# One RWKV-7 layer with its feed-forward network: new durations and offsets for the list scheduler, and new tile sizes

## The chip, the cores and the metric

The program runs on one core of a Trainium2 chip. The metric is the device time of one execution in microseconds (us). The kernel before took 2997.66 us in the median of three runs (2985.98 to 2998.62).

A core has five engines that are spoken of here: TensorE (PE in the profile; its weight loads are PEld), VectorE (DVE), ScalarE (ACT), GpSimd (POOL) and SyncE (SP), which issues most of the DMA transfers. Each engine works its own list of instructions in order, and waits for the others by semaphores. SBUF is the on-chip memory: 128 partitions, and a tile has the same byte address in each of its partitions. PSUM holds the results of PE.

## The reference

One layer over 2048 tokens of width 1024: RWKV-7 time mixing with 16 heads of 64, a layer norm, a gated feed-forward network (FFN) of width 2816 with a causal convolution of width 3, and a second layer norm.

```python
def step(state, inp):                       # per head, 64 x 64, one token after the other
    r_t, w_t, k_t, v_t, kk_t, a_t = inp
    sa = jnp.einsum('bhij,bhj->bhi', state, -kk_t)
    state = (state * w_t[:, :, None, :] + sa[..., None] * (kk_t * a_t)[:, :, None, :]
             + v_t[..., None] * k_t[:, :, None, :])
    return state, jnp.einsum('bhij,bhj->bhi', state, r_t)

# mixed = ((head_norm(y) + bonus) * gate) @ w_o
x = _layer_norm(DEEPNORM_ALPHA * x + mixed, ln1_g[i], ln1_b[i])
# hdn = conv3(x @ w_in) + conv_b; u, g = split(hdn); ffn = (silu(g) * u) @ w_out
x = _layer_norm(DEEPNORM_ALPHA * x + ffn, ln2_g[i], ln2_b[i])
```

`r`, `k` and `v` are projections of the token-shifted input with 1024 x 1024 weights; the decay `w`, `a` and the gate come from low-rank pairs. All data are fp32.

## The kernel before

**Arithmetic.** A large fp32 product is made of three matmuls in the type fp32r on a high and a low part of each operand: `mm3` (L139 to L143) issues high by high (L141), high by low (L142 or L143) and low by high. In the profile such a matmul is `out<-weights,moving`, or with the two names the other way round. Each takes 128 x 128 weights and streams 512 columns.

**Stages.** One list of nodes holds the whole kernel:

- stage A (0 to about 700 us): projections k, r and v with their low-rank parts. A weight matrix is held in two column halves: half h = 0 in the pool `a_w0`, half h = 1 in `a_w1`. A group of PE is 24 matmuls `ps<-WH,xiH`, `ps<-WL,xiH`, `ps<-WH,xiL`.
- recurrence (about 690 to 1294 us): 16 chunks of 128 tokens, in two halves of the heads and two subchunks of 64 tokens. For each half: a load `l`, a cumulative sum `csI` on PE, exponentials `P`, `Pe`, `Pi` on ACT (L823), products `l<-l,P` (L845), `l<-l,Pe` (L841) and `BKn` (L891) on DVE, transposes `tb` (L899), the Gram products `G` on PE and their masking `Gm` (L917). Then the triangular inversion of the chunk: 31 steps on DVE, each a product `itmp` (L949) and a subtraction `XU` (L954). Its result goes to DRAM (`XD`) and back transposed (`XT`), and `X` (L983) feeds the merge on PE (`mp`). The state goes through `UV`, `Z`, `Zs`, `SA`, `dS`, and is updated on DVE by `stmp` (L1098) and `state` (L1103).
- group norm, gate and output projection (about 1293 to 1503 us), 16 token tiles of 128: sums of squares on ACT (`junk`, L1241, 16 for each tile), rsqrt on DVE, the gate product `wE` (L1270, L1273), transposes to `yE` or `yH`/`yL`, and groups of 24 matmuls `z`.
- FFN (1503 to 2978 us): four blocks of 512 tokens; 44 groups of 24 matmuls `ps<-xH,wiH`, `ps<-xL,wiH`, `ps<-xH,wiL` for each block, and 44 groups of 12 matmuls `acc` for each, the second product.

**What sets the order.** Every node is added by `pl.add(engine, duration, priority, function, dependencies, take, give)`. `order()` plays the list through before the program is built: an engine that is free takes the ready node with the smallest priority number whose slots (`take`: buffers and PSUM banks) are free, holds the engine for the duration, and releases dependents after the duration and a fixed latency. The order in which nodes start in this play is the order in which each engine's instructions are written. So the durations, and the priorities, which are a stage's base time plus an offset from the tables `TS` (recurrence) and `TW` (output projection), decide the order, and nothing else; the instructions stay the same. In `TS`, `b` is 23.2 times the chunk number, and the offsets used with it are `inv` (the inversion, L922), `mrg` and `mc` (the merge, L965 and L967), `uv` (the load of `UV`, L1030), `st` and `cs` (the state, L1034); `e0` is taken off for chunk 0. In `TW`, the base is `p0` plus 13 times the token tile, and `st`, `gt`, `tr` and `out` are the offsets of the squares, the gate, the transposes and the output of the layer norm.

**Where the tiles lie.** Tiles come from SBUF pools opened with `tc.tile_pool`, which lays them one behind the other. In the program as built, these are the byte addresses modulo 64 of the operands of the 512-column matmuls: `xH`, `xL`, `xiH`, `xiL` and the weights of half h = 1 in stage A at 0; `wiH`, `wiL`, `woH`, `woL`, `aH`, `aL`, `yH`, `yL` and the weights of half h = 0 at 32; `yE` at 0.

Of the kernel before, what the change touches and what calls it, by code (L numbers as in the profile page):

```python
# [11 lines left out]
F32 = mybir.dt.float32  # L12
# [105 lines left out]
class K:  # L118
# [3 lines left out]

    def ld(self, out, in_):
        return self.nc.sync.dma_start(out, in_)

    st = ld
# [31 lines left out]
    def run(self, phases="ASWF", scratch=None):  # L158
        tc, nc, a = self.tc, self.nc, self.a
        with ExitStack() as ctx:  # L160
# [24 lines left out]
            self.ident = top.tile([128, 128], F32, name="ident")  # L185
# [21 lines left out]
    def a_nodes(self, ctx, pl):  # L207
# [5 lines left out]
        E = lambda **kw: st2.enter_context(tc.tile_pool(reuse_waits="tile", **kw))  # L213
# [8 lines left out]
        E = lambda **kw: st1.enter_context(tc.tile_pool(reuse_waits="tile", side="right", **kw))  # L222
# [41 lines left out]
        for sw, (q, wi, mm, ml) in enumerate((("k", 1, 2, 4), ("r", 0, 0, 1), ("v", 2, 3, 5))):  # L264
# [73 lines left out]
            for h in range(2):  # L338
# [25 lines left out]
                else:  # L364
# [21 lines left out]
                    l2n.append(pl.add("ACT", 0.4, pr + 0.1, fb, [n2], give=("stg",)))  # L386
# [14 lines left out]
            def front(g):  # L401
# [85 lines left out]
                n_l1 = pl.add("PE", 4.33 if q == "v" else 1.93, lp, f_l1, pn + l1n, take=("ph",),  # L487
# [11 lines left out]
                if q == "v":  # L499
# [13 lines left out]
                    n_h = pl.add("ACT", 1.5, lp, f_sg, [n_ha], take=("hid",), give=("ph",))  # L513
                    n_hid = [pl.add("DVE", 0.65, lp, f_gl, [n_h], give=("hz",))]
                else:
# [11 lines left out]
                    n_h = pl.add("ACT", 0.9 if q == "r" else 0.6, lp, f_hid, [n_ha, n_ones], take=("hid",))  # L527
                    n_hid = [n_h, pl.add("DVE", 0.35, lp, f_hl, [n_h], give=("hz",))]
# [7 lines left out]
            for nq, (g, h, tl) in enumerate(order):  # L536
# [6 lines left out]
                if True:  # L543
                    c = slice(h * 512, h * 512 + 512)
                    if True:
# [17 lines left out]
                        if nq < o["ks"][sw] or q == "v" and nq >= len(order) - o["ke"]:  # L563
                            for u in range(3):
                                n_mm = pl.add("PE", 1.29, (wt if sw == 0 else pr) + 0.2 * u, lambda u=u, f=f_mm: f(u),
                                              [n_mm, pn[u], wn[h, 2 * u], wn[h, 2 * u + 1]], take=() if u else (f"pg{pg}",))
                        n_mm = pl.add("PE", 1.29 if n_mm else 5.14, pr, lambda u=3 if n_mm else None, f=f_mm: f(u),
# [15 lines left out]
                        n_l2 = pl.add("PE", 0.86 if q == "v" else 0.43, pr + 0.1, f_l2, n_hid + l2n, take=("pl",),  # L583
# [14 lines left out]
                        if q == "k":  # L598
# [29 lines left out]
                            hn.append(pl.add("ACT", 2.15, po + 0.5, f_ss, [n_kr] + hn))  # L628
# [101 lines left out]
    TS = dict(hf=12, T=23.2, lds=5.0, hs=8.9, inv=31.0, mrg=66.3, mc=4.0, uv=47.5, st=70.2, cs=17.6, e0=30.0, p0=-3.4, fill=(), fn=1,  # L730
# [3 lines left out]
    def s_nodes(self, ctx, pl, n_1, n_2, w, f):  # L734
# [14 lines left out]
        def f_open1():  # L749

            nonlocal inv, wkp, ldp, pw, xui, triI, gmask, cols, gm4, nbI, nbIn, nbE, scE
            E = lambda st=pools1, **kw: st.enter_context(tc.tile_pool(reuse_waits="tile", side="right", **kw))
# [50 lines left out]
        for t in range(NT):  # L803
# [4 lines left out]
            for h in range(2):  # L808
# [47 lines left out]
                n_pp = pl.add("PE", 0.44, hb + 0.7, f_pcp, [n_P, n_R], take=("pw",), give=("P",))  # L856
# [6 lines left out]
                for i, n_x in ((0, n_M), (1, n_R)):  # L863
# [17 lines left out]
                    n_t = pl.add("PE", 0.44, hb + 0.9 + 0.3 * i, f_tr, [n_x], take=("pw",))  # L881
# [4 lines left out]
                for c in range(2):  # L886
# [17 lines left out]
                    n_tb = pl.add("PE", 0.44, hb + 2.0 + c, f_tb, n_bks[2 * c:2 * c + 2], take=("pw",))  # L904
                    n_bt = pl.add("ACT", 0.6, hb + 2.1 + c, f_bt, [n_tb], take=("BKT",), give=("pw",))
# [8 lines left out]
                    n_g = pl.add("PE", 1.05, hb + 2.2 + c, f_g, [n_bt] + evs, take=("pw", "pw"), give=("BKT",))  # L914
# [51 lines left out]
            for c in range(2):  # L966
# [51 lines left out]
                n = pl.add("DVE", 0.67, mc, f_x11, [n_xt], take=("X11",))  # L1018
                n_m1 = pl.add("PE", 0.45, mc, f_m1, [n], take=("mp",), give=("X11",))
                n = pl.add("ACT", 0.6, mc, f_ft, [n_m1], take=("FT",), give=("mp",))  # L1020
                n = pl.add("PE", 0.68, mc, f_m2, [n], take=("mp",), give=("FT",))
                n_x12.append(pl.add("ACT", 0.6, mc, f_x12, [n], give=("mp",)))
                n_ga.append(pl.add("ACT", 1.0, mc + 0.5, f_ga, [n_m1, n_nu]))
# [9 lines left out]
            for c in range(2):  # L1033
# [21 lines left out]
                n_y1 = pl.add("PE", 1.27, sb + 4, f_y1, prevS + evs + ars[0] + [n_z2], take=("Y",))  # L1055
                for u in range(nh):
# [48 lines left out]
                    n_s0 = pl.add("ACT", 1.04 * d, sp, f_s0, (prevS if nh == 1 or len(prevS) < 2 else prevS[u:u + 1]) + [n_uv])  # L1105
                    n_z = pl.add("PE", 1.27 * d, sp, f_z, [n_s0, n_ga[c]], take=bk)
                    n_zs.append(pl.add("ACT", 0.48 * d, sp, f_zs, [n_z, prevA] + n_zs[-1:]))
                    n_sa = pl.add("PE", 1.27 * d, sp, f_sa, n_zs[-1:] + [n_x12[c]], give=(f"XT{c}",) if lastu else ())
                    n_su.append(pl.add("ACT", 0.96 * d, sp, f_su, [n_sa]))
                    n_ds = pl.add("PE", 1.27 * d, sp, f_ds, n_su[-1:])  # L1110
                    n_w.append(pl.add("DVE", 0.6 * d, sp, f_w, [n_ds, *prevS] + n_w[-1:], give=bk))
                    n_s1.append(pl.add("DVE", 0.6 * d, sp, f_s1, n_w[-1:] + n_s1[-1:] + [prevY] + pcs))
                n_y2 = pl.add("PE", 1.27, sb + 4.5, f_y2, n_su + [n_y1] + (n_s1 if c else []),
                              give=("AR", "BKn", "Gm", "PC", "UV") if c else ())
                n_yt = pl.add("ACT", 0.96, sb + 5, f_yt, [n_y2], take=() if c else ("Yt",), give=("Y",))
# [25 lines left out]
    TW = dict(ne=4, st=-31.5, gt=-31.1, tr=-14.5, ld=-22.0, out=26.9, p0=1000.0,  # L1141
# [3 lines left out]
    def w_nodes(self, ctx, pl, n_first, n_ch1, xds, Q, n_rest, stores, f):  # L1145
# [12 lines left out]
        def f_open(early):  # L1158
            E = lambda st=ctx, **kw: st.enter_context(
                tc.tile_pool(reuse_waits="tile", side="right" if early else "left", **kw))  # L1160
# [59 lines left out]
        def loads(t):  # L1220
# [22 lines left out]
            for i in range(8):  # L1243
                n = pl.add("ACT", 0.54, PR(t) + o["st"], lambda i=i: f_ss(i), [n], take=() if i else ("w_q",))
# [42 lines left out]
        def transposes(x, nm, src, pr, deps, early, give=()):  # L1287
            out = []
            for u in range(2):
# [7 lines left out]
                n = pl.add("PE", 0.44, pr + 0.1 * u, f_t, deps + [n_late] * (e == "L") + [n for n, _ in out],  # L1297
# [41 lines left out]
        for t in range(NT):  # L1339
# [4 lines left out]
            for h in range(2):  # L1344
                e = bank("pz", t < 1)
                if t < 2:

                    n = zn[-1][0] if h else None
                    for k in range(KD):
                        n = pl.add("PE", 0.65, pr + 0.1 * k + 5.2 * h,  # L1350
# [3 lines left out]
                else:  # L1354
                    n = pl.add("PE", 5.14, pr + 5.2 * h, lambda t=t, h=h, e=e: [f_mm(t, h, k, e) for k in range(KD)],
# [50 lines left out]
    def f_nodes(self, ctx, pl, Q, n_early, n_w, n_rest, zs, gn, n_sx, n_x1):  # L1406
# [19 lines left out]
        def f_mid():  # L1426
            E = lambda **kw: ctx.enter_context(tc.tile_pool(reuse_waits="tile", side="right", **kw))
# [4 lines left out]
        def f_rest():  # L1432
            E = lambda **kw: ctx.enter_context(tc.tile_pool(reuse_waits="tile", side="left", **kw))
# [28 lines left out]
        for B in range(NB):  # L1462
# [40 lines left out]
            def wout(f, h, pr, mm=True, acc_mm=acc_mm, abank=abank, an=an, accs=accs):  # L1503
# [20 lines left out]
                if 0 < f < NF - 1:  # L1524
                    accs[h] = [pl.add("PE", 2.56, pr, lambda: [acc_mm(f, h, tl, R["H"], R["L"]) for tl in range(4)],
# [3 lines left out]
                for tl in range(4):  # L1529
                    out.append(pl.add("PE", 0.64, pr + 0.1 * tl, lambda tl=tl: acc_mm(f, h, tl, R["H"], R["L"]),  # L1530
# [4 lines left out]
            for f in range(NF):  # L1535
# [3 lines left out]
                for j, fc in enumerate((f, NF + f)):  # L1539
# [24 lines left out]
                    n_mm = pl.add("PE", 5.14, pr, f_mm, [n_w] + xn, take=("w_" + e,), give=("f_wi",))  # L1564
# [128 lines left out]
            for tl in range(4):  # L1693
                n = pl.add("PE", 3.84, pr, lambda tl=tl: [m(tl) for m in mm], nw + [an[f] for f in range(NF)] + [n])
# [69 lines left out]
```

## Time and profile before

| what | value |
|---|---|
| median of three runs | 2997.66 us (2985.98 to 2998.62) |
| the profiled execution's own time | 2995.38 us |
| its span, first to last instruction | 2993.6 us |
| granted PE clock over the span | 0.968 of full speed |
| PE busy | 2828.6 us, 94% |
| DVE busy | 2066.9 us, 69% |
| ACT busy | 1702.8 us, 57% |

The span is what the engines show between their first and last instruction; the 1.8 us around it belong to the execution's time. Busy times are unions over the span, so that overlapping matmuls count once. [...]

### The profile page before, as it was taken

What the parts mean: (1) busy time and instruction counts of PE and PEld (TensorE: products, weight loads), DVE (VectorE), ACT (ScalarE), POOL (GpSimd) and SP (SyncE); (2) the same over time, 40 slices, a digit from 0 to 9 for tenths busy, and PEclk for the clock granted to TensorE, in tenths of its full rate; (3) what the DMA queues carried; (4) which work ended last, traced back from release to release, by engine and by line L of the source; (5) the groups of instructions that cost most, each with busy time, mean ns of one, the idle gap of its engine ahead of it and who ended that gap; (6) DMA issues with size and microseconds to landing.
All of it is one profiled execution on the core that took longest, in us unless ns stands there. A gap on an engine that the chain in (4) does not pass through costs nothing.

```text
span 2993.6 us, 51468 instructions
## 1 busy us (share of the span) xinstructions
PE 2828.6 (94%) x19392; PEld 2290.7 (77%) x19392; DVE 2066.9 (69%) x4160; ACT 1702.8 (57%) x4604; POOL 52.6 (2%) x94
## 2 busy tenths in 40 slices
PE   7999999998788888799999999999999999999997
PEld 5776778886576777678888887888878888888886
DVE  7888768986899888778765555475554744547454
ACT  8888567663576667777554444444444444444441
POOL 0000000001000000001100000000000000000000
PEclk9999999998899889799999999999999999999999
DMA  6346555435555555468553223242232422424222
GB/s 203 140 166 231 174 182 192 145 117 167 146 151 146 151 157 156 119 231 286 199 179 99 91 93 126 95 147 97 94 124 95 151 92 88 129 94 157 89 87 78
DMA packets 267319, 424.04 MB, mean 142 GB/s; under 512 B 120672, under 2 KB 146272, under 8 KB 262976
## 3 DMA queue, kind: packets, MB, share of 16 engines
q1 hardware_dynamic: 255744, 379.87, 40.2%
q0 software_dynamic: 11328, 40.90, 3.8%
q8 instruction: 152, 2.49, 0.4%
q14 instruction: 95, 0.78, 0.1%
HBM read 311.57 MB, written 109.12 MB: 141 GB/s over the span
## 4 chain that ended last, share of the span: by engine, by line
issue 55%; PE 20%; DVE 10%; ACT 8%; DMA 5%; POOL 1%; SPq 0%; POOLq 0%; ACTq 0%; DVEq 0%
PE ps L141 4%; PE ps L142 4%; PE ps L143 4%; ACT junk L619 3%; DVE BKn L891 2%; DMA l<-in 1%; DVE itmp L949 1%; DVE XU L954 1%; PE G L744 1%; DVE Gm L917 1%; DMA NU<-Gm 1%; DMA NUs<-NU 1%; DMA stg<-in_w_rkv_dram 1%; PE csI L744 1%; ACT UV L743 1%
## 5 line engine op out<-in xcount | busy, mean ns | idle before, releaser
L143 PE MATMUL ps<-xH,wiL 128*128 128x512 f32 x1408 | 557.8, 396 | 0.5 <-DVE wiL L1552 0.4
L141 PE MATMUL ps<-xH,wiH 128*128 128x512 f32 x1408 | 556.8, 395 | 0.0
L142 PE MATMUL ps<-xL,wiH 128*128 128x512 f32 x1408 | 556.7, 395 | 0.0
L1552 DVE TENSOR_TENSOR wiL<-wis,wiH 128x1024 fp32r<-128x1024 f32 x176 | 215.4, 1224 | 488.2 <-ACT wiH L1413 488.2
L1413 ACT ACTIVATE hb<-ps 128x512 f32<-128x512 f32 x176 | 105.6, 600 | 518.2 <-PE ps L143 518.2
L141 PE MATMUL ps<-WH,xiH 128*128 128x512 f32 x768 | 307.7, 401 | 15.5 <-ACT xiH L231 10.0
L143 PEld LDWEIGHTS ps<-xH,wiL 128*128 128x128 f32 x1408 | 264.6, 188 | 65.6 <-DVE wiL L1552 2.1
L142 PEld LDWEIGHTS ps<-xL,wiH 128*128 128x128 f32 x1408 | 264.4, 188 | 63.7
L141 PEld LDWEIGHTS ps<-xH,wiH 128*128 128x128 f32 x1408 | 264.5, 188 | 62.9
L142 PE MATMUL ps<-WL,xiH 128*128 128x512 f32 x768 | 305.2, 397 | 2.0 <-DVE WL L326 2.0
L143 PE MATMUL ps<-WH,xiL 128*128 128x512 f32 x768 | 304.9, 397 | 0.0
L1580 DVE SCALAR_TENSOR_TENSOR cv<-hb,cw,cv 128x512 f32<-128x512 f32 x352 | 263.5, 749 | 20.7 <-ACT cv L1576 14.5
L142 PE MATMUL acc<-woL,aH 128*128 128x512 f32 x688 | 269.2, 391 | 1.6 <-DVE woL L1517 1.6
L143 PE MATMUL acc<-woH,aL 128*128 128x512 f32 x688 | 269.8, 392 | 0.0
L141 PE MATMUL acc<-woH,aH 128*128 128x512 f32 x688 | 268.4, 390 | 0.0
L1413 ACT ACTIVATE wiH<-wis 128x1024 fp32r<-128x1024 f32 x178 | 188.8, 1061 | 4.6 <-DMA wis<-in_w_in_dram 4.6
L141 PEld LDWEIGHTS ps<-WH,xiH 128*128 128x128 f32 x768 | 146.7, 191 | 55.4 <-ACT xiH L231 10.0
L142 PEld LDWEIGHTS ps<-WL,xiH 128*128 128x128 f32 x768 | 146.8, 191 | 34.7 <-DVE WL L326 2.5
L1413 ACT ACTIVATE woH<-wos 128x512 fp32r<-128x512 f32 x172 | 108.7, 633 | 113.0 <-PE acc L143 110.5
L143 PEld LDWEIGHTS ps<-WH,xiL 128*128 128x128 f32 x768 | 146.3, 191 | 33.6 <-DVE xiL L450 0.2
L142 PEld LDWEIGHTS acc<-woL,aH 128*128 128x128 f32 x688 | 129.1, 188 | 32.4 <-DVE woL L1517 3.1
L141 PEld LDWEIGHTS acc<-woH,aH 128*128 128x128 f32 x688 | 129.2, 188 | 29.1 <-ACT woH L1413 0.5
(242 smaller groups left out, 5229.4 us busy)
## 6 DMA issues: line engine op xcount, KB each, us to landing
wis<-in_w_in_dram SPq DMA_DIRECT2D x176, 512.0 KB
wos<-in_w_out_dram SPq DMA_DIRECT2D x172, 256.0 KB
l<-in SPq DMA_DIRECT2D x32, 1280.0 KB
xT<-in_xT_dram SPq DMA_DIRECT2D x21, 1028.0 KB
in<-kp SPq DMA_DIRECT2D x64, 256.0 KB
stg<-in_w_rkv_dram SPq DMA_DIRECT2D x48, 256.0 KB
gs<-gs SPq DMA_DIRECT2D x24, 512.0 KB
in<-kr SPq DMA_DIRECT2D x32, 256.0 KB
```

The source lines that it names most:

```text
L141: nc.tensor.matmul(ps, lH, rH, start=start, stop=False)
L142: nc.tensor.matmul(ps, lH, rL, start=False, stop=False)
L143: nc.tensor.matmul(ps, lL, rH, start=False, stop=stop)
L619: nc.scalar.activation(junk, Z["kr"][:, 64 * i:64 * i + 64], AF.Square, accum_out=st["ss"][:, tl, i:i + 1])
L743: CP = lambda out, in_, **kw: nc.scalar.activation(out, in_, AF.Copy, **kw)
L744: MM = lambda out, l, r, **kw: nc.tensor.matmul(out, l, r, **{**dict(start=True, stop=True), **kw}, skip_group_check=True)
L891: TT(dst, l[es(c), 1 if part else 3], V[t]["Pi", h][es(c)], op=OP.mult)
L917: TT(V[t]["Gm"][:, e, c, 4 * h:4 * h + 4], V[t]["G", h, c, e], gm4, op=OP.mult)
L949: TT(V[t]["tv"], V[t]["XU"][:, 0:m, s:s + 1].to_broadcast([128, m, n]), V[t]["NUs"][:, s:s + 1, s + 1:32].to_broadcast([128, m, n]), op=OP ...
L1413: CP = lambda out, in_, **kw: nc.scalar.activation(out, in_, AF.Copy, **kw)
L1552: TT(W["L"], W["s"], W["H"], op=OP.subtract)
L1580: STT(R[j], W["hb"][:, i:i + 512], C["cw"][:, fc, i:i + 1], R[j], op0=OP.mult, op1=OP.add)
```

## The change

It has three parts, and no instruction is added or taken away.

1. The durations in the `pl.add` calls are set to other numbers.
2. Offsets in `TS` and `TW` are set to other numbers.
3. All SBUF pools of the four stages go through a new class, `Pool64`, that rounds the size of each tile up to a multiple of 64 bytes; `ident` becomes columns 8 to 136 of a tile of 136.

```diff
+class Pool64:
+    def __init__(self, pool):
+        self.pool = pool
+
+    def tile(self, shape, dtype, **kw):
+        n = math.prod(shape[1:])
+        if n % 16 == 0:
+            return self.pool.tile(shape, dtype, **kw)
+        x = self.pool.tile([shape[0], -(-n // 16) * 16], dtype, **kw)[:, 0:n]
...
+        return x
...
+    def pool(self, st, **kw):
+        p = st.enter_context(self.tc.tile_pool(**kw))
+        return p if kw.get("space") is not None else Pool64(p)
...
-            self.ident = top.tile([128, 128], F32, name="ident")
+
+            self.ident = top.tile([128, 136], F32, name="ident")[:, 8:136]
...
-        E = lambda **kw: st2.enter_context(tc.tile_pool(reuse_waits="tile", **kw))
+        E = lambda **kw: self.pool(st2, reuse_waits="tile", **kw)
...
-    TS = dict(hf=12, T=23.2, lds=5.0, hs=8.9, inv=31.0, mrg=66.3, mc=4.0, uv=47.5, st=70.2, cs=17.6, e0=30.0, p0=-3.4, fill=(), fn=1,
+    TS = dict(hf=12, T=23.2, lds=5.0, hs=8.9, inv=28.74, mrg=95.85, mc=6.68, uv=51.49, st=70.2, cs=17.6, e0=40.21, p0=-3.71, fill=(), fn=1,
...
-                n_y1 = pl.add("PE", 1.27, sb + 4, f_y1, prevS + evs + ars[0] + [n_z2], take=("Y",))
+                n_y1 = pl.add("PE", 1.08, sb + 4, f_y1, prevS + evs + ars[0] + [n_z2], take=("Y",))
...
-    TW = dict(ne=4, st=-31.5, gt=-31.1, tr=-14.5, ld=-22.0, out=26.9, p0=1000.0,
+    TW = dict(ne=4, st=-25.05, gt=-23.51, tr=-12.52, ld=-22.0, out=31.18, p0=1000.0,
...
-                n = pl.add("ACT", 0.54, PR(t) + o["st"], lambda i=i: f_ss(i), [n], take=() if i else ("w_q",))
+                n = pl.add("ACT", 0.75, PR(t) + o["st"], lambda i=i: f_ss(i), [n], take=() if i else ("w_q",))
```

In the changed program as built, every operand of the 512-column matmuls lies at 32 modulo 64. Modulo 128, `xH` and `wiH` are 64 bytes apart, and so are the pairs of `ps<-WH,xiH` in half h = 0; the pairs in half h = 1 are level.

The line numbers of the changed kernel are 21 or 22 higher, so the pieces of the two orders stand apart. First DVE in the second half of chunk 11 (`X` and `state` belong to chunks 9 and 8, `itmp` and `XU` to the inversion of chunk 10; a number behind a name is the buffer's). Before:

```order
L949 TENSOR_TENSOR itmp<-XU,NUs 128x120
L1098 TENSOR_TENSOR stmp<-dS,state 128x512
L954 TENSOR_TENSOR XU<-XU,itmp 128x6x20
L1103 TENSOR_TENSOR state<-stmp,PC 128x512
L949 TENSOR_TENSOR itmp<-XU,NUs 128x133
L983 STREAM_TRANSPOSE X_13185<-XT_7821 32x256 x2
L917 TENSOR_TENSOR Gm<-G,c_gmask 128x512 x4
L954 TENSOR_TENSOR XU<-XU,itmp 128x7x19
L983 STREAM_TRANSPOSE X_13253<-XT_7822 32x256 x2
```

The same place in the changed program:

```order
L1125 TENSOR_TENSOR state<-stmp,PC 128x512
L971 TENSOR_TENSOR itmp<-XU,NUs 128x126
L976 TENSOR_TENSOR XU<-XU,itmp 128x6x21
L939 TENSOR_TENSOR Gm<-G,c_gmask 128x512
L971 TENSOR_TENSOR itmp<-XU,NUs 128x120
L939 TENSOR_TENSOR Gm<-G,c_gmask 128x512
L976 TENSOR_TENSOR XU<-XU,itmp 128x6x20
L939 TENSOR_TENSOR Gm<-G,c_gmask 128x512
L971 TENSOR_TENSOR itmp<-XU,NUs 128x133
L939 TENSOR_TENSOR Gm<-G,c_gmask 128x512
L976 TENSOR_TENSOR XU<-XU,itmp 128x7x19
L1005 STREAM_TRANSPOSE X_13211<-XT_7821 32x256 x2
```

The four masks `Gm` stand between inversion steps now, not in one piece, and the transposes `X` behind them instead of ahead.

Next ACT at the end of the recurrence, from the scaling of the state of chunk 14 on (`junk` are the squares of the group norm of the first token tiles). Before:

```order
L743 ACTIVATE UV<-state 64x4x64 x2
L1241 ACTIVATE junk,q<-wE 128x64 x4
L743 ACTIVATE Yt<-Y_15885 64x8x64 x2
L743 ACTIVATE Zs<-Z 128x256
L743 ACTIVATE UV<-state 64x4x64 x2
L1241 ACTIVATE junk,q<-wE 128x64 x6
L743 ACTIVATE UV<-SA 64x4x64 x2
L1241 ACTIVATE junk,q<-wE 128x64 x2
L743 ACTIVATE Zs<-Z 128x256
L1241 ACTIVATE junk,q<-wE 128x64 x6
L743 ACTIVATE UV<-SA 64x4x64 x2
```

The same place in the changed program:

```order
L765 ACTIVATE UV<-state 64x4x64 x2
L765 ACTIVATE Yt<-Y_15897 64x8x64 x2
L765 ACTIVATE Zs<-Z 128x256
L765 ACTIVATE UV<-state 64x4x64 x2
L1262 ACTIVATE junk,q<-wE 128x64 x2
L1235 ACTIVATE woH_15968<-wos 128x512
L765 ACTIVATE UV<-SA 64x4x64 x2
L765 ACTIVATE Zs<-Z 128x256
L1262 ACTIVATE junk,q<-wE 128x64 x2
L1235 ACTIVATE woH_15979<-wos 128x512
L765 ACTIVATE UV<-SA 64x4x64 x2
```

Where 14 squares stood between the copies up to the second `UV<-SA`, 4 stand now, and two conversions of the output weights (`woH`) with them; the other squares come later.

Last DVE at the end of the recurrence, from the last `X` on, where `wE` is the gate product of token tile 0. Before:

```order
L983 STREAM_TRANSPOSE X_16358<-XT_7822 32x256 x2
L1270 TENSOR_TENSOR wE<-wE,rn 128x1024
L1215 TENSOR_TENSOR woL_16003<-wos,woH_16002 128x512
L1273 TENSOR_TENSOR wE<-wE 128x1024
L1215 TENSOR_TENSOR woL_16160<-wos,woH_16159 128x512
L1273 TENSOR_TENSOR wE<-wE 128x1024
L1253 TENSOR_SCALAR q<-q 128x16
```

In the changed program the piece with the last `stmp` is this:

```order
L1236 TENSOR_TENSOR woL_16256<-wos,woH_16255 128x512
L1120 TENSOR_TENSOR stmp<-dS,state 128x256
L1125 TENSOR_TENSOR state<-stmp,PC 128x256
L1236 TENSOR_TENSOR woL_16283<-wos,woH_16282 128x512
L1120 TENSOR_TENSOR stmp<-dS,state 128x256
L1274 TENSOR_SCALAR q<-q 128x16
L171 TENSOR_SCALAR rsw<-q 128x16
L172 TENSOR_SCALAR rsy<-rsw 128x16
```

Before, the rsqrt and the gate of token tile 0 stood ahead of the last four `stmp`; now the rsqrt of tile 0 (`q`, `rsw`, `rsy`) begins behind the last `stmp`, and its gate behind the last `state`. On PE, so, no transpose of `wE` and no `z` stands ahead of the last products of the recurrence any more, where up to 16 transposes and the first `z` stood.

## Rows read from the trace of the kernel before

**Rows 1.** Windows: stretch, length, busy us (instructions) by engine, granted PE clock, DMA share, GB/s.

```profile
300.00:700.00 400.00, 399.08 (x1935) 328.21 (x1934) 317.68 (x622) 256.32 (x936) 3.49 (x7) 1.00 0.48 162
800.00:1200.00 400.00, 338.74 (x6552) 278.13 (x6548) 354.68 (x1074) 274.17 (x567) 6.39 (x12) 0.91 0.55 152
1200.00:1300.00 100.00, 77.07 (x1595) 67.63 (x1596) 70.46 (x224) 77.17 (x223) 5.37 (x10) 0.78 0.51 140
1300.00:1500.00 200.00, 195.27 (x958) 162.16 (x957) 162.66 (x379) 135.48 (x582) 20.56 (x30) 0.99 0.71 241
1503.00:2977.40 1474.40, 1472.25 (x6352) 1190.51 (x6350) 821.50 (x1087) 657.12 (x1263) 9.72 (x17) 1.00 0.34 110
```

**Rows 2.** Timeline of PE in the FFN: start, us, engine, line, operation, tiles, shapes.

```profile
1701.61 0.40 PE L143 MATMUL ps<-xH,wiL 128*128 128x512 f32 x1
...
1707.91 0.40 PE L143 MATMUL ps<-xH,wiL 128*128 128x512 f32 x1
1708.14 0.39 PE L141 MATMUL acc<-woH,aH 128*128 128x512 f32 x1
...
1710.65 0.39 PE L143 MATMUL acc<-woH,aL 128*128 128x512 f32 x1
```

**Rows 3.** Timeline of PE in stage A: a group of h = 0, then one of h = 1.

```profile
505.04 0.40 PE L141 MATMUL ps<-WH,xiH 128*128 128x512 f32 x1
...
510.40 0.40 PE L143 MATMUL ps<-WH,xiL 128*128 128x512 f32 x1
516.26 0.40 PE L141 MATMUL ps<-WH,xiH 128*128 128x512 f32 x1
...
521.48 0.39 PE L143 MATMUL ps<-WH,xiL 128*128 128x512 f32 x1
```

**Rows 4.** Timeline of PE in the output projection: tile yE, then tile yH.

```profile
1296.74 0.39 PE L142 MATMUL z<-woL,yE 128*128 128x512 f32 x1
...
1299.07 0.39 PE L143 MATMUL z<-woH,yE 128*128 128x512 f32 x1
1365.03 0.39 PE L143 MATMUL z<-woH,yL 128*128 128x512 f32 x1
...
1369.81 0.40 PE L143 MATMUL z<-woH,yL 128*128 128x512 f32 x1
```

**Rows 5.** Page, part 5: groups by line: xcount, busy us and mean ns of one, idle before.

```profile
L143 PE MATMUL ps<-xH,wiL 128*128 128x512 f32 x1408 | 557.8, 396 | 0.5 <-DVE wiL L1552 0.4
L141 PE MATMUL ps<-WH,xiH 128*128 128x512 f32 x768 | 307.7, 401 | 15.5 <-ACT xiH L231 10.0
```

**Rows 6.** Timeline of DVE: the state update of one subchunk, nine chunks apart.

```profile
861.01 0.68 DVE L1103 TENSOR_TENSOR state<-stmp,PC 128x512 f32<-128x512 f32 x1
...
1163.20 0.68 DVE L1103 TENSOR_TENSOR state<-stmp,PC 128x512 f32<-128x512 f32 x1
```

**Rows 7.** Waits of DVE, 800 to 1200 us: line, releaser, us in total, times, longest.

```profile
DVE l L845 <- ACT P L823: 11.9, 14, 2.3
DVE Gm L917 <- PE G L744: 9.0, 14, 1.2
```

**Rows 8.** Waits of PE in the same stretch.

```profile
PE mp L744 <- DVE X L983: 4.1, 4, 2.5
```

**Rows 9.** Chain that ended last, 1240 to 1300 us: start, us, what.

```profile
1239.94 7.15 DMA XT<-XD
...
1293.35 0.43 PE z L141
```

**Rows 10.** Groups of ACT, 1250 to 1273 us, by line and shape.

```profile
L1241 ACT ACTIVATE junk<-wE 128x64 f32<-128x64 f32 x28 | 7.2, 256 | 0.8
L1241 ACT ACTIVATION_READ_ACCUMULATOR junk<-wE 128x1 f32 x28 | 5.2, 187 | 0.0
```

**Rows 11.** Timeline of DVE, end of the recurrence: the gate of token tile 0, the last `stmp`.

```profile
1272.76 1.23 DVE L1270 TENSOR_TENSOR wE<-wE,rn 128x1024 f32<-128x1024 f32 x1
...
1293.40 0.42 DVE L1098 TENSOR_TENSOR stmp<-dS,state 128x256 f32<-128x256 f32 x1 [1.10 <-PE dS L744]
```

More of the change, by code (lines that the diff above doesn't have):

```diff
@@ L33, in bc_rows @@
     return bass.AP(tensor=ap.tensor, offset=ap.offset, ap=[[0, n], [1, ap.shape[-1]]])
+class Pool64:
[6 more added lines that the diff above has]
+        x = self.pool.tile([shape[0], -(-n // 16) * 16], dtype, **kw)[:, 0:n]
+        if len(shape) > 2:
+            d = " ".join(f"d{i}" for i in range(1, len(shape)))
+            x = x.rearrange(f"p ({d}) -> p {d}", **{f"d{i}": shape[i] for i in range(2, len(shape))})
+        return x
 class Node:
@@ L220, in a_nodes @@
         plp = E(name="a_pl", bufs=sl["pl"], space=PSUM)
-        E = lambda **kw: st1.enter_context(tc.tile_pool(reuse_waits="tile", side="right", **kw))
+        E = lambda **kw: self.pool(st1, reuse_waits="tile", side="right", **kw)
         lp1 = E(name="a_l1", bufs=1)
@@ L512, in f_gl @@
                         TT(X["gR"][32:64], X["hz"][0:32], X["gR"][0:32], op=OP.subtract)
-                    n_h = pl.add("ACT", 1.5, lp, f_sg, [n_ha], take=("hid",), give=("ph",))
-                    n_hid = [pl.add("DVE", 0.65, lp, f_gl, [n_h], give=("hz",))]
+                    n_h = pl.add("ACT", 1.76, lp, f_sg, [n_ha], take=("hid",), give=("ph",))
+                    n_hid = [pl.add("DVE", 0.88, lp, f_gl, [n_h], give=("hz",))]
                 else:
@@ L526, in f_hl @@
                         TT(X["hid"][64:128], X["hz"], X["hid"][0:64], op=OP.subtract)
-                    n_h = pl.add("ACT", 0.9 if q == "r" else 0.6, lp, f_hid, [n_ha, n_ones], take=("hid",))
-                    n_hid = [n_h, pl.add("DVE", 0.35, lp, f_hl, [n_h], give=("hz",))]
+                    n_h = pl.add("ACT", 1.07 if q == "r" else 0.62, lp, f_hid, [n_ha, n_ones], take=("hid",))
+                    n_hid = [n_h, pl.add("DVE", 0.45, lp, f_hl, [n_h], give=("hz",))]
                 pn = pm or prep("m", mm, gb + o["mm"], ("xT",))
@@ L1017, in f_ga @@
                         CP(V[t]["Gm"][0:64, e, c, :, 0:64], V[t]["AR"][es(e), c, :, 0])
[L1018 to L1023, printed above, removed]
+                n = pl.add("DVE", 0.93, mc, f_x11, [n_xt], take=("X11",))
+                n_m1 = pl.add("PE", 0.62, mc, f_m1, [n], take=("mp",), give=("X11",))
+                n = pl.add("ACT", 0.79, mc, f_ft, [n_m1], take=("FT",), give=("mp",))
+                n = pl.add("PE", 0.62, mc, f_m2, [n], take=("mp",), give=("FT",))
+                n_x12.append(pl.add("ACT", 0.77, mc, f_x12, [n], give=("mp",)))
+                n_ga.append(pl.add("ACT", 1.28, mc + 0.5, f_ga, [n_m1, n_nu]))
             def f_uv(t=t):
@@ L1158, in f_open @@
         def f_open(early):
-            E = lambda st=ctx, **kw: st.enter_context(
-                tc.tile_pool(reuse_waits="tile", side="right" if early else "left", **kw))
+            E = lambda st=ctx, **kw: self.pool(st, reuse_waits="tile", side="right" if early else "left", **kw)
             if early:
@@ L1426, in f_mid @@
         def f_mid():
-            E = lambda **kw: ctx.enter_context(tc.tile_pool(reuse_waits="tile", side="right", **kw))
+            E = lambda **kw: self.pool(ctx, reuse_waits="tile", side="right", **kw)
             Q["wk"] = E(name="f_wk", bufs=2)
```

74 lines of the change are left out of this document (37 added, 37 removed).

## The prediction

> **What bounds the kernel now.** I read the windows by stage first, and there PE's busy time against the stretch. In the FFN PE is busy for 1472.25 of 1474.4 us, in the second half of stage A for 399.08 of 400, in the output projection for 195.27 of 200, all at a granted clock of 0.99 to 1.00; in the recurrence it is busy for 338.74 of 400 at 0.91, beside DVE with 354.68 [rows 1]. So in three stages the spacing of the matmuls is the time, and in the recurrence no engine is full: there DVE is the fullest, and 45.3 of its 400 us are idle.
>
> Then I read the spacing in the timeline of PE, since the bounded stages are made of one shape, 128x512. In the FFN 27 spacings of `ps` take 6.30 us, 233.3 ns each; the 11 spacings of `acc` right behind take 2.51 us, 228.2 ns [rows 2]. The clock is the same and so is the shape. In stage A a group of h = 0 has 23 spacings in 5.36 us, 233.0 ns, and a group of h = 1, the same line of code and the same names, 23 in 5.22 us, 227.0 ns [rows 3]. In the output projection the products with `yE` take 233.0 ns (10 spacings in 2.33 us), those with `yH` and `yL` 227.6 (21 in 4.78) [rows 4]. That makes three slow rows and three fast ones. What divides them is where the two operands lie modulo 64 bytes: `xH` at 0 with `wiH` at 32, the weights of h = 0 at 32 with `xiH` at 0, `woH` at 32 with `yE` at 0 are slow; `acc` and `yH` (32 and 32) and h = 1 (0 and 0) are fast. I take this as the reading: operands at unequal places modulo 64 cost 5 to 6 ns for each matmul of 512 columns. It is worked out from pairs of tiles; no row moves one tile alone.
>
> [...]
>
> **The change part by part.** The sum stands against the profiled execution, 2995.38 us (span 2993.6); the median of the runs is 2.3 us above it, and they scatter over 12.6 us.
>
> *Tile sizes, FFN.* There are 3 x 1408 = 4224 matmuls `ps` [rows 5]. With `xH` and `wiH` both at 32 modulo 64 they should go at the spacing of `acc`, 228.2 ns, which like them has operands at 32 modulo 64: 4224 x (233.3 - 228.2) = -21.5 us. PE is full there, and nothing else ends the stage, so it counts whole. As a check, 4224 x 0.2333 + 2112 x 0.2282 = 1467 us of the stage's 1474. Ends: at the 227.0 ns of rows 3 it is -26.6, and 0 if placement does nothing.
>
> *Tile sizes, stage A.* Half of the 3 x 768 = 2304 matmuls [rows 5], 1152, are of half h = 0: 1152 x (233.0 - 228.2) = -5.5 us. Two thirds of them, r and v, lie where PE is full [rows 1]; in k, the first third, PE also waits for loads and conversions, and I count nothing. That is -3.7, between 0 and 1152 x 6.0 = -6.9. The half h = 1 moves from 0 to 32 as a pair and stays as it is. The output projection's four tiles with `yE` give 96 x 5.4 ns = -0.5. The sizes of tiles change no DVE or ACT instruction, and I count none there: the cover is that DVE and ACT are not full where PE is.
>
> *Order in the recurrence.* Nine chunks take from 861.01 to 1163.20 us, 33.6 each [rows 6]. DVE's named waits there are led by `l` for the exponential `P` (11.9 us in 400) and by `Gm` for the Gram products `G` (9.0, 14 times) [rows 7]. In the new order each `Gm` has an inversion step ahead of it, which needs no PE, so the next product has some 0.5 us more to come. I take the wait for `G` as gone: 9.0 x 500/400 for the stretch from 700 to 1200 us, -11. The wait for `P` I leave: in both orders `l` stands behind a load, `csI` on PE and `P` on ACT, and what is late next after `G` is this chain. Best end: all of DVE's idle 45.3 us, -57 over 500 us. Worst end: the slower rival, +43. I take the value near the row of `Gm`, because that is the only wait whose cover I see in the order.
>
> *Order at the end of the recurrence.* ACT is on the chain there, between two transfers and PE's products [rows 9], and runs 28 squares in 23 us: 7.2 + 5.2 = 12.4 us [rows 10]. In the piece shown 14 become 4, so of the 12.4 us some 10/14 go, -8.9, and two conversions of about 0.6 come in: -7.7. Behind ACT the next to be late are PE's products and the `stmp` on DVE, so I take -6, between 0 and -9. The squares are not gone: they come later, and so does what needs them.
>
> *Start of the output projection.* Now the first `z` starts at 1293.35 [rows 9], as the last `stmp` begins at 1293.40 [rows 11]. In the new order the rsqrt of token tile 0 comes behind that `stmp`, then its three gate products of 1.23 us [rows 11], the transposes and the sum with the bonus. The products alone are 3.7 us; for the rsqrt and the transposes I allow once to twice as much again, so the start moves by 3.7 to 11 us, and I take +7. Part of it could be covered, as PE has 4.7 us idle in the following 200 [rows 1]; I do not count on that.
>
> Sum: -21.5 - 3.7 - 0.5 - 11 - 6 + 7 = -35.7, 2995.4 - 36 = 2959 us.
>
> **The rivals.**
>
> *Placement does nothing.* The spacing would belong to how these tiles are written or loaded, and be the same after. For it: the trace has no row in which one operand alone moved. Against it: three pairs of rows with one divider. Then 2995.4 - 11 - 6 + 7 = 2985. [...]
>
> *Slower: the merge waits for the inversion.* The result of the inversion goes through DRAM, and the way back alone takes 7.15 us [rows 9]. PE waits only 4.1 us in 400 for `X` now, 4 times [rows 8]; `X` comes behind the four `Gm` in the new order, and PE works its list in order, so that `csI` of the next half, queued behind `mp`, would be late with it, then `P`, then `l` on DVE. If the wait grows by 3.3 us in each of 13 chunks, that is +43: 2995.4 - 25.7 + 43 + 1 = 3014. It eats the gain of placement from 2.0 us a chunk on (25.7/13). Against it: DVE, not PE, is the fuller engine, and the `Gm` ahead of `X` are four pieces of 0.7 us.
>
> *The recurrence gains more.* DVE's idle time falls by 32 of its 45.3 us in 400: -40 over 500, and 2995.4 - 25.7 - 40 + 1 = 2931. For it: the durations that set the order are changed throughout, so more waits than the one for `G` may go. Against it: the wait for `P` hangs on a loop through SP, PE, ACT and DVE that has not become shorter.
>
> *Only the late start shows.* The end of the recurrence gains nothing, the new order of the recurrence nothing, and the output projection starts 11 us later: 2995.4 - 25.7 + 11 = 2981.
>
> **How the numbers follow.** Forecast 0.56, with its own range 2945 to 2972; placement without effect 0.10; slower 0.04; more in the recurrence 0.20; only the late start 0.10. The range from 2925 to 2985 leaves out the slower case, half of the one without placement, and the lower part of the gain in the recurrence, some 0.15 together. A measurement here can tell about 0.5%, 15 us. Faster by more than that (under 2982.7) are the forecast, the gain in the recurrence, most of the late start and a part of the case without placement: 0.85. Within it 0.11, slower 0.04.
>
> **What would show it.** In the profile after: 27 spacings of `ps` in the FFN in about 6.16 us instead of 6.30, and the FFN some 21 us shorter from the first `ps` to the last `acc`; groups of h = 0 in stage A as fast as those of h = 1; chunks of about 32.8 us with the wait of `Gm` for `G` near 0; ACT's squares outside the last two chunks; the first `z` some 7 us behind the last `stmp`. The prediction is wrong if `ps` stays at 233 ns, or if the chunks are longer than 33.6 us by 2 or more with `mp` waiting for `X`.

## The result and the profile after

The changed kernel takes 3032.79 us in the median of four runs (3029.3 to 3041.63), the kernel before 2998.14 (2985.98 to 3003.22): a ratio of 1.0126, 95% interval 1.0088 to 1.0164. It is slower by 35 us; 2959 us had been forecast, with a range up to 2985. The profiled execution is the longest of the four, 3041.63 us with a span of 3039.8, 46 us over the span before.

The windows of the changed kernel, by stages as in [rows 1] (columns as there; the later stretches are shifted to where those stages lie now):

```profile
300.00:700.00 400.00, 398.37 (x1913) 326.70 (x1914) 317.23 (x620) 252.36 (x899) 1.87 (x4) 1.00 0.48 165
800.00:1200.00 400.00, 335.08 (x6522) 276.97 (x6523) 342.64 (x1063) 273.62 (x554) 5.86 (x11) 0.89 0.54 148
1326.50:1533.30 206.80, 204.60 (x1000) 169.16 (x999) 169.64 (x386) 139.51 (x598) 21.64 (x32) 0.99 0.73 250
1533.30:3023.20 1489.90, 1478.51 (x6356) 1194.26 (x6354) 822.81 (x1087) 657.01 (x1263) 10.07 (x17) 1.00 0.33 109
```

In the stretches shown of the three bounded stages PE is nearly as full as before, except in the FFN: there it stands idle for 11.4 of 1490 us, where it was 2 of 1474 [rows 1]. Then the spacing, from one start to the next, which carried most of the forecast, in the timeline of PE of the changed kernel: 25 spacings of `ps` in the FFN with the `acc` behind them, and a group of half h = 0 in stage A (columns: start, us, engine, line, operation, tiles, shapes).

```profile
1733.12 0.40 PE L163 MATMUL ps<-xL,wiH 128*128 128x512 f32 x1
...
1738.95 0.39 PE L164 MATMUL ps<-xH,wiL 128*128 128x512 f32 x1
1739.19 0.39 PE L162 MATMUL acc<-woH,aH 128*128 128x512 f32 x1
...
1741.70 0.39 PE L164 MATMUL acc<-woH,aL 128*128 128x512 f32 x1
```

```profile
522.32 0.39 PE L162 MATMUL ps<-WH,xiH 128*128 128x512 f32 x1
...
527.68 0.40 PE L164 MATMUL ps<-WH,xiL 128*128 128x512 f32 x1
```

25 spacings in 5.83 us are 233.2 ns, as before [rows 2]; `acc` has 228.2, as before; h = 0 has 23 in 5.36 us, 233.0, as in [rows 3]. The new tile sizes did not move the spacings that were to fall. Next the state update of DVE nine chunks apart, then DVE's waits from 800 to 1200 us (line, releaser, us in total, times, longest), both of the changed kernel, and last, from the same stretch, the wait for `NUs` before and PE's wait of `csI` for the load `l`, before and after:

```profile
888.59 0.68 DVE L1125 TENSOR_TENSOR state<-stmp,PC 128x512 f32<-128x512 f32 x1
...
1191.76 0.68 DVE L1125 TENSOR_TENSOR state<-stmp,PC 128x512 f32<-128x512 f32 x1
```

```profile
DVE l L867 <- ACT P L845: 17.2, 8, 3.5
DVE itmp L971 <- DMA NUs<-NU: 9.0, 6, 2.9
DVE Gm L939 <- PE G L766: 4.1, 2, 2.9
```

```profile
DVE itmp L949 <- DMA NUs<-NU: 0.9, 2, 0.6
PE csI L744 <- DMA l<-in: 2.9, 4, 1.2
PE csI L766 <- DMA l<-in: 16.4, 9, 4.3
```

The wait of `Gm` for `G` fell from 9.0 us [rows 7] to 4.1, but the chunk takes 33.7 us against 33.6 [rows 6]: the wait for the transfer `NUs` rose from 0.9 to 9.0, and the one for `P` from 11.9 to 17.2. On PE `csI`, which stands ahead of `P`, waits 16.4 us for the load `l`, where it was 2.9. The end of the recurrence is next, first DVE, then PE, both as timelines of the changed kernel (in brackets the idle time ahead and its releaser):

```profile
1314.93 0.42 DVE L1120 TENSOR_TENSOR stmp<-dS,state 128x256 f32<-128x256 f32 x1 [0.72 <-PE dS L766]
1315.27 0.17 DVE L1274 TENSOR_SCALAR q<-q 128x16 f32<-128x16 f32 x1
...
1317.99 1.22 DVE L1291 TENSOR_TENSOR wE<-wE,rn 128x1024 f32<-128x1024 f32 x1
...
1321.47 1.22 DVE L1294 TENSOR_TENSOR wE<-wE 128x1024 f32<-128x1024 f32 x1
```

```profile
1322.74 1.11 PE L1317 MATMUL tr<-ident,wE 128*128 128x128 f32 x4 [6.92 <-DVE wE L1294]
...
1326.49 0.78 PE L162 MATMUL z<-woH,yE 128*128 128x512 f32 x1
1327.06 0.63 PE L163 MATMUL z<-woL,yE 128*128 128x512 f32 x1
1327.49 0.63 PE L164 MATMUL z<-woH,yE 128*128 128x512 f32 x1
```

From the state update at 1191.76 to the last `stmp` at 1314.93 it takes 123.2 us, where it was 130.2 [rows 6, 11]. The first `z` comes 11.6 us behind the last `stmp`, where the two began together [rows 9, 11].

The 46 us of the profiled pair, stage by stage (from the first and last rows of the tiles named; A is the end of the last `ps<-W`):

| stretch | before | after | change |
|---|---|---|---|
| start to A | 714.6 | 730.9 | +16.3 |
| A to the first state update of rows 6 | 146.4 | 157.7 | +11.3 |
| nine chunks | 302.2 | 303.2 | +1.0 |
| to the last `stmp` | 130.2 | 123.2 | -7.0 |
| last `stmp` to first `z` | -0.1 | 11.6 | +11.6 |
| first `z` to end of `z` | 209.2 | 206.8 | -2.4 |
| end of `z` to end of `acc` | 1474.9 | 1489.9 | +15.0 |

The second row I take as scatter of this one execution, since with the same order of the recurrence that stretch took 147.5 us in e2 and 151.9 in e7; no run isolates it. Two of the three large losses, stage A and the FFN, lie in stages that the prediction had priced by the spacing alone.

Stage A loses most of its time, 11.2 of 16.3 us, in one place, the change from the projection k to r. These windows hold the same 120 matmuls of PE, first of the kernel before, then of the changed one:

```profile
284.20:310.00 25.80, 25.80 (x120) 20.06 (x119) 23.35 (x48) 17.15 (x38) 0.00 (x0) 1.00 0.87 295
```

```profile
287.60:324.60 37.00, 30.31 (x120) 22.45 (x120) 32.41 (x65) 22.86 (x53) 0.00 (x0) 0.82 0.81 265
```

25.8 us became 37.0, and the granted clock 0.82: PE stands idle for 6.7 us, and the same 120 matmuls keep it busy for 30.3 us in place of 25.8. PE's waits there in the changed kernel:

```profile
PE p L603 <- DVE gH L548: 4.4, 1, 4.4
PE p L603 <- ACT w L659: 1.4, 2, 1.1
```

`gH`, the hidden tile of the low-rank part, comes late. In the FFN nearly all of PE's idle time has one releaser; its waits in the changed kernel, and the first of the three long ones on DVE and on PE:

```profile
PE acc L163 <- DVE woL L1538: 10.9, 6, 3.5
```

```profile
2034.83 1.23 DVE L1632 TENSOR_TENSOR xr<-xr,ag 128x1024 f32<-128x1024 f32 x1
2038.00 1.23 DVE L1632 TENSOR_TENSOR xr<-xr,ag 128x1024 f32<-128x1024 f32 x1 [1.95 <-DMA xr<-xn]
2039.14 1.22 DVE L1633 TENSOR_TENSOR xr<-xr,ab 128x1024 f32<-128x1024 f32 x1
2040.28 0.68 DVE L1538 TENSOR_TENSOR woL<-wos,woH 128x512 fp32r<-128x512 f32 x1
```

```profile
2041.02 0.80 PE L163 MATMUL acc<-woL,aH 128*128 128x512 f32 x1 [3.15 <-DVE woL L1538]
```

DVE's list has the products `xr` for the next layer norm ahead of `woL`. The second `xr` waits 1.95 us for its transfer, 2.4 us of work follow, and `acc` waits 3.15 us for `woL`.

### The profile page after: what moved, and what is told of

Read it like the earlier page. It is cut to its first block, busy times and chain, and to the rows that moved or that the text cites. A ratio compares the mean times of both kernels' runs of the same rounds, so it can differ in the third digit from the quotient of the medians.

```text
span 3039.8 us, 51455 instructions
## 1 busy us (share of the span) xinstructions
PE 2843.7 (94%) x19392; PEld 2296.4 (76%) x19392; DVE 2064.0 (68%) x4160; ACT 1704.0 (56%) x4604; POOL 52.6 (2%) x94
## 4 chain that ended last, share of the span: by engine, by line
issue 55%; PE 20%; DVE 11%; DMA 8%; ACT 5%; POOL 1%; SPq 1%; POOLq 0%; DVEq 0%; ACTq 0%
PE ps L162 4%; PE ps L163 4%; PE ps L164 4%; DMA in<-av 1%; DMA l<-in 1%; DVE Gm L939 1%; DVE BKn L913 1%; DVE XU L976 1%; DVE itmp L971 1%; ACT junk L641 1%; PE G L766 1%; DMA stg<-in_w_rkv_dram 1%; DMA NU<-Gm 1%; DMA NUs<-NU 1%; PE mp L766 1%
## 5 line engine op out<-in xcount | busy, mean ns | idle before, releaser
L163 PE MATMUL acc<-woL,aH 128*128 128x512 f32 x688 | 272.4, 396 | 10.9 <-DVE woL L1538 10.9
```

The source lines that it names most:

```text
L163: nc.tensor.matmul(ps, lH, rL, start=False, stop=False)
```

## The experiments

Theory A: the loss comes from the new order, and placement does nothing. Its rival B: the new places cost time and the order gains as forecast. The first four kernels take the change apart.

**e1, tile sizes alone.** Edit: `Pool64`, the calls of it and `ident` added to the kernel before.

> The kernel before with the tile sizes of the change alone (Pool64 and ident); durations, offsets and so the order stay. Theory A (the change is slower by its order; placement does nothing): 2998 us, within 8, and in the trace ps of the FFN and of h = 0 at 233 ns, h = 1 at 227, as before. Theory B (the new places cost time themselves, and the order gains as forecast): 3030 us or more. The prediction's own step (unequal places modulo 64 cost 5 us per 1000 matmuls) would give 2972.

Measured: 3006.06 us against 3002.53, ratio 1.0010 (0.9993 to 1.0027). A group of `ps` of the FFN in its timeline of PE:

```profile
1723.64 0.39 PE L162 MATMUL ps<-xH,wiH 128*128 128x512 f32 x1
...
1729.00 0.39 PE L164 MATMUL ps<-xH,wiL 128*128 128x512 f32 x1
```

23 spacings in 5.36 us, 233.0 ns. B falls, and so does the prediction's step on placement.

**e2, order alone.** Edit: `Pool64` and `ident` taken back out of the changed kernel.

> The changed kernel without its tile sizes: new durations and offsets, old places. Theory A: 3033 us, within 8, with the stages' lengths of the changed kernel (stage A 16 us longer than before, first z some 10 us later against the last state, FFN 10 to 15 us longer). Theory B: 2985 us.

Measured: 3029.47 us, ratio 1.0084 (1.0057 to 1.0112). Stage A ends at 732.3 us, the first `z` comes 10 us later against the last state, the FFN takes 1488.4 us. The order carries the loss (the whole change has 1.0126, and the two intervals overlap).

**e3, durations alone, and e4, offsets alone.** Edits: the rows `TS` and `TW` of before put into e2; those of after put into before.

> New durations, old offsets, old places. Theory A1 (the durations reorder stage A and the FFN, which have no new offsets, and that is most of the loss): 3022 to 3030 us, with stage A 16 us and the FFN 10 to 15 us longer than before, and a recurrence that is off by up to 10 either way. Theory A2 (the offsets carry the loss): 3000 us, within 8.

> New offsets, old durations, old places. Theory A1: stage A and FFN as before, the recurrence and the start of the output projection 10 to 17 us later: 3008 to 3015 us. Theory A2: 3030 us.

Measured: e3 3048.65 us, ratio 1.0145 (1.0112 to 1.0178), stage A to 731.4 us, FFN 1490.6; e4 3011.04, ratio 1.0022 (1.0006 to 1.0038), stage A to 716.7, FFN 1476.0. The durations carry more than the whole loss, more than was expected of them. The new offsets alone cost a little, and not where A1 put it: the first `z` comes 5 us ahead of the last `stmp`, not later, and the `z` then take 215.9 us in place of 209.2. With the new durations the offsets give some 20 us back.

**e5, the spacing by itself.** Edit: the whole work replaced by 64 segments of this kind, with `so` and `mo` the places of weights and streamed operand.

```python
for i in range(48):
    k = i % 8
    nc.tensor.matmul(ps, s[:, so + 128 * k:so + 128 * k + 128], m[:, mo + 512 * k:mo + 512 * k + 512],
                     start=i == 0, stop=i == 47)
```

> Not the layer: 64 segments of 48 matmuls 128x512 in fp32r, weights and streamed operand in one tile each, and nothing else of weight; the output is filled with the last segment. The weights lie 0 to 480 bytes further (steps of 32) for each of four places of the streamed operand (0, 32, 128 and 256 bytes further). Theory P (the distance of the two operands modulo 256 bytes decides, which the traces of before and after allow): at the same distance the same spacing for all four places, some distances at 227 to 229 ns and others, among them 32, 192 and 224 counted from weights to streamed operand, at 233. Theory Q (placement never mattered; something else belongs to those tiles): one spacing for all, within 1.5 ns.

Its timeline of PE (start, us of the 48 together, tiles): the weights are moved by 0, 32, 64, ... bytes from `p_aa` to `p_ai`, so that the streamed operand is 0, 224, 192, ... modulo 256 ahead of them.

```profile
54.68 11.05 PE L142 MATMUL p_aa<-m,s 128*128 128x512 f32 x48
65.57 11.35 PE L142 MATMUL p_ab<-m,s 128*128 128x512 f32 x48
...
87.96 11.40 PE L142 MATMUL p_ad<-m,s 128*128 128x512 f32 x48
...
121.56 11.16 PE L142 MATMUL p_ag<-m,s 128*128 128x512 f32 x48
...
143.75 11.05 PE L142 MATMUL p_ai<-m,s 128*128 128x512 f32 x48
```

48 matmuls take 11.05 us or up to 11.40, by the distance alone. The mean spacings of the one execution, from the first start of a segment to its last (47 spacings); they are the same for all four places within 0.5 ns at distance 0 and 0.1 ns elsewhere, and the same again 256 bytes on:

| streamed operand minus weights, modulo 256 | 0 | 32 | 64 | 96 | 128 | 160 | 192 | 224 |
|---|---|---|---|---|---|---|---|---|
| ns | 226.9 | 233.4 | 229.0 | 233.4 | 232.5 | 234.2 | 233.4 | 233.2 |

So theory P holds, in a form that neither theory nor prediction had: only 0 (226.9 ns) and 64 (229.0) are fast. In the kernel before as built `xH` is 224 ahead of `wiH`, in the changed one 192: slow both times, 233.3 [rows 2] and 233.2 ns.

**e6, the distance set to 0.** Edit, on the kernel before:

```diff
+        E(name="a_gap", bufs=1).tile([128, 56], F32, name="gap")
         wps[0] = E(name="a_w0", bufs=1)
...
+                    Q["fc"].tile([128, 56], F32, name="gap")
                     Q["wi"] = E(name="f_wi", bufs=2)
+                    E(name="f_gap", bufs=1).tile([128, 8], F32, name="gap")
```

> The kernel before with three unused tiles of 224, 224 and 32 bytes, so that xH and xL lie at the same place modulo 256 as wiH and wiL, and the weights of h = 0 at the same as xiH and xiL; nothing else moves modulo 256. Theory P: ps of the FFN and of h = 0 at 227 to 229 ns instead of 233, 4224 x 5 ns + some 4 us: 20 to 28 us faster than before, ratio 0.991 to 0.993. Theory Q: as before, ratio 0.998 to 1.002.

Measured: 2983.34 us against 3005.73, ratio 0.9935 (0.9915 to 0.9954), 20 us. A group of `ps` of the FFN in its timeline of PE:

```profile
1710.67 0.39 PE L142 MATMUL ps<-xH,wiH 128*128 128x512 f32 x1
...
1715.88 0.40 PE L144 MATMUL ps<-xH,wiL 128*128 128x512 f32 x1
```

23 spacings in 5.21 us, 226.5 ns; the FFN takes 1457.0 us, 17.9 less. The mean of all `ps` spacings there, waits left out, is 228.0 ns (233.3 before), which for 4224 of them would be 22 us; that of `acc`, which was not to change, went from 228.7 to 229.5 and gives nearly 2 us of that back. With the 2.1 us of stage A the gain stands at the lower end of the range expected. So the place of two operands against each other does set the spacing, 226.5 ns here and 233.0 in e1; the distances that the change sets are not the fast ones.

**e7, recurrence and output projection alone, and e8, recurrence alone.** Edits: e2 with the numbers of before in stage A and FFN, and in e8 also in the output projection and `TW`.

> New durations and new offsets for the recurrence and the output projection alone; stage A and the FFN keep the old durations, all places are old. If the loss of the new order lies in stage A (+17 us) and the FFN (+14), this is 30 us below the new order whole: about 2997 us, ratio 0.997, with a recurrence some 8 us shorter than before and the first z 8 us behind the last state. If the stages do not separate (the list of one shifts the other), 3010 us or more.

> New durations and offsets for the recurrence alone; stage A, output projection and FFN are old. If the late start of the output projection comes from its own new durations and offsets, the first z comes as before about 1 us ahead of the last state's end, and the kernel is 8 us faster than before, ratio 0.997; if it comes from the recurrence's, the first z stays 8 us behind and the ratio is 1.000.

Measured: e7 3001.41 us, ratio 0.9988 (0.9977 to 1.0000); e8 3010.88, ratio 1.0027 (1.0011 to 1.0043). The stages separate. In e8 the first `z` is still 10 us behind the last state and the `z` take 213.8 us (206.2 in e7): the late start comes from the recurrence's numbers, and the output projection's own make up for 7 us of it.

**e9, the best of both.** Edit: e6's three tiles in e7.

> The three spacer tiles of e6 together with the new durations and offsets of recurrence and output projection of e7; stage A and FFN keep the old durations. If the two are independent, 0.9935 x 0.9988 = 0.992, some 2982 us, 20 us or more below before and 45 to 50 below the changed kernel. If the new order of the recurrence only shifts waits that the faster FFN brings back, 0.9935.

Measured: 2975.52 us against 3001.93, ratio 0.9907 (0.9892 to 0.9922): 28 us faster than before by the ratio, and 53 us faster than e2 (0.9907 against 1.0084, of 3002 us). The 0.992 of two independent gains lies within the interval.

**e10 and e14, the FFN's loss.** Edit: the FFN's new durations in the kernel before, and the two products `xr` (L1632 and L1633 of the changed kernel) at `fb + 24` in e10, `fb + 70` in e14, instead of `fb + 8`.

> New durations in the FFN alone (those of the changed kernel), and the products xr with the layer norm's factors get the offset fb + 24 instead of fb + 8, so that woL stands ahead of them on DVE at the blocks' ends. Theory W (the FFN's loss is acc waiting for woL, which is queued behind an xr that waits for its transfer): the three waits of 3 to 4 us go, the FFN takes 1474 to 1480 us instead of 1488 to 1491, ratio 1.000 to 1.002. Theory V (the new durations make the FFN longer elsewhere): 1488 us, ratio 1.005.

> As e10, with fb + 70 for the xr products. Theory W (all of the FFN's loss is acc waiting for woL behind xr): acc's long waits fall below the 14.3 us of e10, toward the 3.6 of before, and the FFN takes 1474 to 1479 us. Theory U (with the new durations the back-to-back acc groups wait for woL whatever stands there): 1482 us or more.

Measured: e10 1482.5 us of FFN, ratio 1.0040 (1.0025 to 1.0054), half of the loss gone and between the two theories; e14 1474.3 us, ratio 0.9988 (0.9970 to 1.0007). PE's wait in the FFN of e14:

```profile
PE acc L163 <- DVE woL L1537: 1.1, 2, 0.9
```

1.1 us, where the changed kernel had 10.9, e10 6.3 and the kernel before 1.6. With the new durations kept and `xr` behind `woL` the whole loss is gone: shown.

**e11, e12 and e13, stage A's loss.** Edits in the kernel before: PE's new durations in stage A (e11); `pl.add("ACT", 2.91, po + 0.5, f_ss, ...)` for 2.15 (e12); all new durations of stage A with `lp - 10` for the nodes behind `gH` (e13).

> In stage A alone the new durations of PE's nodes (5.46 for 5.14, 1.36 for 1.29, 1.88 and 4.67 for the low-rank ones, 0.45 and 0.91); ACT's and DVE's are old, and so is all the rest. If PE's durations cause the delay at the change from k to r: stage A ends at 728 to 733 us instead of 715, ratio 1.005. If ACT's do: 715 us, ratio 1.000.

> In stage A alone the new duration of the sums of squares of kr on ACT (2.91 for 2.15); all the rest is old. If ACT's share causes the delay at the change from k to r: stage A ends at 728 to 733 us, ratio 1.005. If PE's durations do: 715 us, ratio 1.000.

> All new durations in stage A, the rest old, and the nodes of the low-rank hidden tile (hz, the activation, gH) get an offset that is 10 lower, so that fewer xif stand ahead of gH on DVE and ACT. Theory G (the loss is PE waiting for gH behind xif at the change from k to r): stage A ends at 715 to 722 us, ratio 1.000 to 1.002. Theory H (the loss is spread over stage A's order): 728 to 735 us, ratio 1.004 to 1.006.

Measured: stage A ends at 723.2, 718.5 and 728.0 us (714.6 before, 732.3 in e2); ratios 1.0035 (1.0023 to 1.0048), 1.0020 (1.0002 to 1.0037) and 1.0033 (1.0013 to 1.0053). No single duration is the cause. PE's waits at the same place, one of e12, then two of e13:

```profile
PE p L602 <- DVE gH L547: 4.9, 1, 4.9
```

```profile
PE p L602 <- ACT w L658: 6.6, 2, 4.0
PE ps L162 <- DVE av L668: 3.7, 1, 3.7
```

In e12 the wait for `gH` is as long as in the changed kernel, and the stage ends only 3.9 us later than before; in e13 it is gone, others of 6.6 and 3.7 us stand in its place, and the stage ends 13.4 us later. So theory G falls. H's length holds at the bottom of its range (728.0 us, its ratio just under it), but the time is still lost at the change from k to r, not spread. That stage A loses at the change from k to r is shown, and that its durations do it; which instruction of ACT's or DVE's order holds the rest stays open.

## Why the prediction was wrong

**Placement (-21.5, -3.7, -0.5): 0.** The step that failed is "What divides them is where the two operands lie modulo 64 bytes". Six groups of tiles agreed with it, but the same six agree with "0 or 64 modulo 256, counted from the weights": the slow pairs are 32 apart modulo 64, so never at 0 or 64, and the fast pairs, at 227.0 to 228.2 ns [rows 2, 3, 4], lie near the 226.9 and 229.0 that e5 shows only there. The prediction did write that no row moved one tile alone; it should have priced what that leaves: under the other reading the FFN's pair goes from 224 to 192 and nothing happens. The rival "placement does nothing" named the right outcome for this term with a wrong reason. In e5 the spacing goes from 226.9 to 234.2 ns by the distance alone. What makes the distance count, no run here shows.

**Order in the recurrence (-11): 0.** The wait for `G` halved, as argued, and two others took its place: the one for `P` (+5.3 us in 400), which the sentence on what is late next had named, and the one for `NUs` (+8.1), which the prediction did not have. The term counted the first wait and not what came behind it. In the profiled runs nine chunks take 296 to 306 us with the old order of the recurrence (eight kernels) and 298 to 303 with the new (five).

**End of the recurrence (-6): -7 in the profiled pair, -9 in the means.** From the later state update of [rows 6] to the last one it takes 123 to 127 us in those five kernels, 131 to 135 in the eight. The size was right, the mechanism only for a part. Here are ACT's squares between the eighth state update from the end and the last one (columns as in [rows 1], of the tile `junk` alone, two instructions for each square): before, changed, e3, e8.

```profile
1253.69:1294.34 40.65, 11.15 (x64) 0.73 0.42 123
1284.30:1317.66 33.36, 8.52 (x50) 0.91 0.25 65
1284.16:1319.59 35.43, 11.08 (x64) 0.80 0.14 32
1259.35:1295.06 35.71, 11.16 (x64) 0.79 0.14 32
```

e3 and e8 have all 32 squares of before there, and still take 5 us less; the 7 squares fewer of the changed kernel go with 2 us more. What else left the stretch in these three kernels are the 12 transposes of `wE`, the first `z` and three copies to `yE` on ACT, all work of the output projection. In e4, where they stay beside 38 squares, it takes 42.3 us. So most of this gain goes with the move that makes the output projection start late (no run makes that move alone), and that the squares, priced at nearly the whole, came out at the right size was luck. (The piece that was counted has 18 squares up to the second `UV<-SA`, not 14.)

**Late start (+7): +11.6, of which 2 to 4 came back** in the `z` (206.8 us against 209.2, and the first of them ran at a granted clock of 0.50, below). The mechanism was right; the size lies a little above the 11 us that were the upper end.

**Not in the sum: stage A, +16, and FFN, +15.** These are two thirds of the 46 us, and the second step that failed: the prediction put the new order of these stages at nothing, without a reason. It read the order at the recurrence and its end, because those had new offsets, and counted the stages in which PE is full at the spacing only. But a stretch that PE fills, as the 25.80 of 25.80 us above, has nothing to gain from an order and much to lose, and e3 shows that the durations alone lose it. Some of the new durations are nearer to the traces (24 `ps` at 233 ns take 5.6 us; their node went from 5.14 to 5.47), and still the order is worse, since work with slack came ahead of work that PE waits for: `xr` ahead of `woL`, as e14 shows. "Slower: the merge waits for the inversion" had the right sign with the wrong place. PE's wait for `X` from 800 to 1200 us in the changed kernel, where it was 4.1 [rows 8]:

```profile
PE mp L766 <- DVE X L1005: 0.2, 1, 0.2
```

## What to carry to other kernels

A pattern read from a handful of tile pairs is a guess until one tile is moved alone: before it is paid for, list the other rules that fit the same rows and what each makes of the change. Where matmuls of one shape stand back to back, set the distance of their two operands and measure it: here three unused tiles of 480 bytes together were worth 20 us, more than the best order alone (e7, some 4 us, barely clear of the noise). And when a scheduler's durations change, read the order of every stage, first of those where an engine is full: there a new order has little to win.

## What the runs showed of the hardware

In e5 the spacing of fp32r matmuls of 512 columns with new weights for each followed the distance of streamed operand and weights modulo 256 bytes: 226.9 ns at 0, 229.0 at 64, 232.5 to 234.2 at the six others tried, at all four places of the streamed operand (granted clock 0.986 over the span of 792.4 us).

After the late start PE's granted clock was down, 0.50 from 1322.7 to 1330.9 us. PE had been idle for 6.92 us ahead of the first transpose, as the timeline above shows, and the matmuls behind `z` started 0.43 us apart in place of 0.23. The window of the changed kernel from the first `z` on, and the eleventh `z` in the timeline:

```profile
1326.50:1336.90 10.40, 8.95 (x34) 6.72 (x33) 6.08 (x10) 4.59 (x17) 1.08 (x2) 0.79 0.97 363
1330.90 0.42 PE L163 MATMUL z<-woL,yE 128*128 128x512 f32 x1
```

The granted 0.79 is a mean: in windows of the changed kernel the clock is 0.50 from 1326.5 to 1330.9 us and 1.00 from there to 1336.9. From the first `z` at 1326.49 to the eleventh ten spacings take 4.41 us; at the 0.233 us of `yE` in [rows 4] they would take 2.33, so by estimate some 2 us are the clock's. At the change from k to r in stage A the granted clock is 0.82 over 37 us, where it was 1.00, and the same 120 matmuls keep PE busy for 4.5 us longer. In both places the wait of PE came with a lower clock, and cost more than itself.
